# The last four tiles of experts' rows by one-hot products, and low-rank weights split ahead of time

## The chip, the cores and the metric

The kernel runs on one core of a Trainium2 chip. The metric is device time in microseconds (us), the median of several executions. Engines: TensorE (PE) multiplies matrices, VectorE (DVE), ScalarE (ACT) and GpSimd (POOL) work on elements, SyncE (SP) mostly issues DMAs. Each engine takes its instructions in the order in which they were written for it; waits between engines are semaphores. DMAs can be issued from SP, ACT and POOL.

## The reference, cut to what matters

Two blocks follow each other on 512 tokens of width 1024. The first ends with a mixture of experts: 64 experts of inner width 256, 8 for each token, and a shared expert.

```
order = argsort(e_flat); counts per expert padded to blocks of 128 rows
def expert_block(toks, ws, e):
    xb = u_pad[toks]
    hid = silu(xb @ we_gate[e]) * (xb @ we_up[e])
    return (hid @ we_down[e]) * ws[:, None]
routed = segment_sum(y_slots, slot_tok)          # back to tokens
h = h + g2 * (routed + shared)
h = rmsnorm(h, final_norm_g)
```

The second block begins with a time mix. Its decay and rate come through weights of low rank (w1, a1: 1024 to 64 each; w2, a2: 64 to 1024):

```
xn = rms_norm(h, norm_pre)
xmix = xn + (shift(xn) - xn) * mu                # six mixes
r, k, v, g = xmix[:4] @ w_in
w_pre = w0 + tanh(xw @ w1) @ w2
a = sigmoid(a0 + (xa @ a1) @ a2)
```

A recurrence over time, attention and a gated embedding follow; nothing there is changed.

## The kernel before, in words

**Precision.** Most products are made of three: a matrix is split into a high part h (a rounded copy, fp32r, made on ACT) and a low part l = matrix - h (DVE or POOL); `hilo` (L222 to L224) does this. A product is then h x h + h x l + l x h.

**First block.** `first_mix` ends with three products on the branch weights (the last is w_brp, L493) and then with w_out, which feeds the residual `hT` ([128, 8, 512], features on partitions). PE runs without a break there.

**Experts.** `Schedule` lists tiles of 128 rows: one expert, or two half experts with 64 rows each. `Experts.run` (L1303) goes over them in a pipeline: tile i's rows were gathered (POOL) and transposed (`operand`), `gate_up` makes the hidden rows, `hidden` the activation on ACT and DVE, `turned` transposes it, `down` makes 1024 outputs for each row. For most tiles `out` scales the rows by their routing weights into `m_y` and POOL scatters them, added up, to one of two token-ordered buffers in DRAM, `rt_d[0]` and `rt_d[1]`, in turn (L1248; a tile of two halves makes two scatters). A scatter waits until the scatter before it to the same buffer has landed.

A tile with `t.add` (the last two, L1092) goes another way, `parts` (L1252): its scaled rows are split into `yh` (ACT, L1264) and `yl` (DVE, L1265), and a matrix `to` of ones and zeros, from comparing row numbers, says which token each row belongs to (L1261, four instructions). `added` (L1272) multiplies (`yh`, `yl`) with `to` for every tile kept: for two tiles four products for each of the 8 feature slices, 32 in all, each slice added to `hT` by `residual` (L1269, DVE).

**The way back.** At tile N-3, `back` (L1286) issues four SP loads of the two halves of `rt_d[0]` and `rt_d[1]` (1 MB each) into places of experts' weights. Ahead of the last tile's outputs in the code the rest of it runs: DVE and POOL add the two (L1297), PE transposes 32 squares (L1301), DVE adds to `hT`. A loop for surplus blocks (L1386) runs zero times here, but engines pass its branches. After it `added(on_h)` handles the tiles kept, with `Norms.add` squaring each slice (ACT, L1430), summing (PE, L1432), storing `hT` to `h_d` and at the end making the norm factors (DVE L1438 to L1441, POOL L1442).

**Start of the second block.** `rwkv` (L1454) opens pools for its tiles; the first, `wts3`, holds three buffers each of `wr`, `wh`, `wl` (a weight as loaded, its high and its low part), and lies where experts' tiles were. `Pre.lora` (L1604) loads the low-rank weights, multiplies w1 by the mixing factors (DVE, L1623, held by `issue_after` until the norm's last DVE instruction), subtracts (L1624), splits three matrices of 128 x 1024, and then multiplies 48 times (L1633) with the normed `hT` (L1500), whose parts `xh`, `xl` come from ACT and from DVE and POOL in turn. Behind it come the mixes for k and r, `mix` (L1490), and 8 pairs of products for k and r (L1522). Between these, `Pre.stages` sets, for a pair, products on L1703, L1712, L1734 and L1742; L1742 takes `p_bk`, whose last part is DVE's L1722. The weights for these products are loaded by `weights` (L1507) into `wr`.

The code's order is not the order of the engines: the frame around the program runs its own timing of the whole and sets the instructions of each engine from it, so that a change in one stage also moves instructions in others.

## Time and profile before

| what | us |
|---|---|
| median of 3 runs | 2513.7 (2513.29 to 2515.72) |
| the profiled execution | 2504.29 |
| its span (first to last instruction) | 2502.5 |

All rows come from the profiled execution, which was 9.4 us quicker than the median. Its mean granted TensorE clock was 0.957 of full speed. A timeline's row reads: start, duration, engine, line, operation, output and inputs, how many in a row; in brackets the engine's idle time before and who ended it. Line numbers are those of the kernel before; in the new kernel everything from L492 on moves down by 3, from L1286 by 4, from L1341 by 6 and in the second block by 13 to 27.

### The profile page before, as it was taken

To read this page: it belongs to the slowest core of one execution; us is meant where nothing else is said; L and a number is where in the kernel's file an instruction comes from. 1 tells how busy PE (TensorE), PEld (TensorE's weight loads), DVE (VectorE), ACT (ScalarE), POOL (GpSimd) and SP (SyncE) were. 2 spreads that over 40 slices of the span, in tenths; PEclk is the share of its full clock that TensorE was granted. 3 is DMA by queue.
4 is the path that set the end of the run, shared out by engine and by line. 5 is a ranking of instruction groups with operands and counts; after the bars stand their busy time and mean duration, and the time that the engine had idled before them with its cause. 6 is when DMAs were issued, how large, how long until landed. Compare 5 with 4: busy or idle time off the path is not lost. (4 is left out here: it accounts for less than half of the span.)

```text
span 2502.5 us, 31640 instructions
## 1 busy us (share of the span) xinstructions
PE 2283.3 (91%) x11912; PEld 1641.4 (66%) x11912; DVE 1308.8 (52%) x2382; ACT 876.6 (35%) x1597; POOL 771.3 (31%) x596
## 2 busy tenths in 40 slices
PE   6899999998998999999989976998979899999997
PEld 3677888776886544443334335666868798988887
DVE  5567877767643433211111126758525556477765
ACT  3443333343322211111111115535326644354552
POOL 2333434114001122222212224449324221655212
PEclk9899999999999999999999987999979999999998
DMA  7232333344733889999999963576765432122211
GB/s 287 94 101 101 103 108 108 119 145 159 268 101 119 338 302 399 381 347 387 399 382 362 376 203 117 152 187 189 205 175 200 144 105 88 56 60 65 79 65 51
DMA packets 187178, 477.16 MB, mean 191 GB/s; under 512 B 62333, under 2 KB 111869, under 8 KB 146832
## 3 DMA queue, kind: packets, MB, share of 16 engines
q1 hardware_dynamic: 161392, 424.48, 47.1%
q0 software_dynamic: 16288, 37.21, 5.7%
q10 hardware_dynamic: 9344, 13.44, 1.8%
q8 instruction: 94, 1.54, 0.2%
q14 instruction: 60, 0.49, 0.1%
HBM read 423.66 MB, written 71.89 MB: 198 GB/s over the span
## 5 line engine op out<-in xcount | busy, mean ns | idle before, releaser
L224 POOL TENSOR_TENSOR wl<-wr,wh 128x1024 fp32r<-128x1024 f32 x80 | 202.9, 2553 | 373.2 <-ACT wh L223 373.2
L223 ACT ACTIVATE wh<-wr 128x1024 fp32r<-128x1024 f32 (+1 forms) x202 | 204.3, 1043 | 236.1 <-PE mm L205 147.7
L205 PE MATMUL mm<-uh,wh 128*128 128x512 f32 x640 | 258.4, 404 | 10.4 <-DVE cv L604 7.6
L205 PE MATMUL mm<-ul,wh 128*128 128x512 f32 x640 | 256.1, 400 | 0.0
L205 PE MATMUL mm<-uh,wl 128*128 128x512 f32 x640 | 255.7, 400 | 0.0
L1196 PE MATMUL mm<-m_we,m_x 128*64 128x512 f32 (+1 forms) x672 | 250.7, 599 | 0.3 <-DMA m_we<-in_w_exp_dram 0.3
L205 PE MATMUL mm<-ya,wh 128*128 128x256 f32 x1280 | 243.9, 291 | 6.8 <-ACT wh L223 6.7
L205 PEld LDWEIGHTS mm<-ya,wh 128*128 128x128 f32 x1280 | 204.9, 196 | 13.9 <-ACT wh L223 7.9
L224 DVE TENSOR_TENSOR wl<-wr,wh 128x1024 fp32r<-128x1024 f32 (+1 forms) x122 | 154.7, 1286 | 65.6 <-ACT wh L223 65.3
L205 PE MATMUL mm<-ya,wl 128*128 128x256 f32 x640 | 184.6, 289 | 0.0
L1186 DVE COPY m_x<-sm 128x512 f32<-128x512 f32 x48 | 33.2, 691 | 289.5 <-PE mm L1196 226.5
L1196 PE MATMUL mm<-m_wl,m_x 128*64 128x512 f32 (+1 forms) x432 | 169.1, 601 | 5.9 <-DMA m_wl<-in_w_exp_dram 5.9
L1196 PEld LDWEIGHTS mm<-m_we,m_x 128*64 128x64 f32 (+1 forms) x672 | 86.8, 159 | 111.4 <-issue 108.8
L1196 PE MATMUL mm<-m_we,m_ht 128*64 128x512 f32 (+1 forms) x368 | 140.8, 601 | 11.4 <-ACT m_y L1236 6.7
L205 PEld LDWEIGHTS mm<-uh,wh 128*128 128x128 f32 x640 | 122.3, 191 | 41.5 <-issue 8.1
L205 PEld LDWEIGHTS mm<-ul,wh 128*128 128x128 f32 x640 | 122.0, 191 | 29.0 <-issue 0.3
L205 PEld LDWEIGHTS mm<-uh,wl 128*128 128x128 f32 x640 | 121.7, 190 | 29.3
L1169 POOL DMA_INDIRECT m_xg<-u_d,sgi x48 | 50.4, 1050 | 273.5 <-PE sm L1184 81.1
L205 PEld LDWEIGHTS mm<-ya,wl 128*128 128x128 f32 x640 | 125.3, 196 | 0.5
L1522 PE MATMUL mm<-xh,wh 128*128 128x512 f32 x256 | 106.3, 418 | 5.7 <-ACT xh L223 3.4
L1248 POOL DMA_INDIRECT rt_d<-m_y,sgi x46 | 70.9, 1542 | 125.0 <-ACT m_y L1236 35.2
L1522 PE MATMUL mm<-xl,wh 128*128 128x512 f32 x256 | 105.6, 413 | 4.0 <-DVE xl L224 2.8
(575 smaller groups left out, 4839.9 us busy)
## 6 DMA issues: line engine op xcount, KB each, us to landing
m_we<-in_w_exp_dram SPq DMA_DIRECT2D x117, 1024.0 KB
m_wl<-in_w_exp_dram SPq DMA_DIRECT2D x78, 1024.0 KB
wr<-in_w_grp_dram SPq DMA_DIRECT2D x32, 1024.0 KB
wr<-in_w_ada_dram SPq DMA_DIRECT2D x18, 1024.0 KB
ck<-pk_d SPq DMA_DIRECT2D x16, 1024.0 KB
csb<-cs_d ACTq DMA_DIRECT2D x16, 512.0 KB
wr<-in_w_pg_dram SPq DMA_DIRECT2D x8, 1024.0 KB
raw<-in_w_ada_dram SPq DMA_DIRECT2D x6, 1024.0 KB
```

The lines of the kernel that those rows point to most:

```text
L205: nc.tensor.matmul(pt, lhsT=l, rhs=r, start=n == 0, stop=n == last)
L223: self.nc.scalar.activation(hi, src, AF.Copy)
L224: return (eng or self.nc.vector).tensor_sub(lo, src, hi.bitcast(F32)).ins
L1169: self.g.nc.gpsimd.indirect_dma_start(out=xg, out_offset=None, in_=self.u2_d, bounds_check=511, oob_is_err=False, in_offset=bass.IndirectO ...
L1186: nc.vector.tensor_copy(x[:, 4:], v_(p, 4))
L1196: self.mark = self.g.nc.tensor.matmul(p[s], lhsT=x[:, s], rhs=w, start=start, stop=stop).ins
L1248: nc.gpsimd.indirect_dma_start(out=self.rt_d[self.turn], out_offset=bass.IndirectOffsetOnAxis(ap=ix, axis=0), in_=y[:ix.shape[0]], in_offs ...
L1522: nc.tensor.matmul(p, lhsT=a_[:, s], rhs=b_, start=k == 0 and i == 0, stop=k == 7 and i == 2)
```

## The change

There are three parts. **First**, four tiles instead of two get `t.add`; when the loop is at tile N-2, ahead of the way back's second half, `added()` brings in tiles N-4 and N-3, and the list is emptied. **Second**, `lora_weights` prepares all low-rank parts in the first block, between w_brp and w_out, with POOL and ACT, and stores six matrices (0.5 MB each) to `lw_d` in DRAM from POOL; `Pre.lora` only loads them, from POOL. **Third**, `Experts.tile` gives `hid`, `ht` and `to` to the pool `wp`, and only `x` to `xp`; and in `rwkv` the pool `rp` is opened ahead of `wts3`. The places of `wr`, `wh` and `wl` are then others.

```
@@ -177,6 +177,7 @@
         self.ps = pool("ps", 1, space=PSUM)
         self.last = None
         self.e_d = self.dram.tile([2, 8, P, 512], F32, name="e_d")
+        self.lw_d = self.dram.tile([6, P, 1024], F32R, name="lw_d")
 
     def acc(self, n=512):
         return self.ps.tile([P, 512], F32, tag="mm", name="mm", bufs=3)
@@ -491,6 +492,8 @@
             g.linear(pk("w_gs"), uh, ul, on_gs)
             g.linear(pk("w_gp"), uh, ul, on_gp)
             g.linear(pk("w_brp"), mh, ml, on_yp)
+        with tc.tile_pool(name="lorw", bufs=1, reuse_waits="tile") as sp:
+            lora_weights(g, sp)
         xs = {}
         sp = st.enter_context(tc.tile_pool(name="sq", bufs=1, reuse_waits="tile", side="right"))
         sq = [sp.tile([P, 512], F32, name="sq%d" % i) for i in range(2)]
@@ -1089,7 +1092,7 @@
         for _, x in sorted(place(full) + place(three) + place(mixed), key=lambda x: x[0]):
             for y in x:
                 add(*y)
-        for t in self.tiles[-2:]:
+        for t in self.tiles[-4:]:
             t.add = True
         self.slot, self.aux = {}, aux
         keys = [t.key for t in self.tiles if t.key]
@@ -1124,7 +1127,7 @@
         self.raw, self.xg, self.us, self.turn = {}, {}, [], 0
 
     def tile(self, n, w, bufs, dt=F32):
-        return self.xp.tile([P, w], dt, tag="m_" + n, name="m_" + n, bufs=bufs)
+        return (self.xp if n == "x" else self.wp).tile([P, w], dt, tag="m_" + n, name="m_" + n, bufs=bufs)
 
     def y(self, dt=F32):
         return self.wp.tile([P, 1024], dt, tag="m_y", name="m_y", bufs=5)
@@ -1282,6 +1285,7 @@
                 if m % 2 == 0:
                     t = self.x_tile()
                 on_h(m, t[:, 512 * (m % 2):512 * (m % 2) + 512])
+        self.add = []
 
     def back(self):
 
@@ -1338,6 +1342,8 @@
             if i + 1 < N:
                 p = g.acc()
                 gate_up(p, i + 1, 0)
+            if whole and i == N - 2:
+                self.added()
             if whole and i == N - 1:
                 drain(bk)
             t = self.turned(hid)
@@ -1406,6 +1412,27 @@
     return [g.a[n][i].rearrange("p m k c -> p (m k c)") for i in range(2)]
 
 
+def lora_weights(g, sp):
+
+
+    nc, a = g.nc, g.a
+    t = lambda n, b, dt=F32: sp.tile([P, 1024], dt, tag=n, name=n, bufs=b)
+    w1, wb, w2 = t("w1", 1), t("wb", 1), t("w2", 1)
+    nc.sync.dma_start(out=w1, in_=a["w_l1"])
+    for j in range(2):
+        nc.sync.dma_start(out=w2[64 * j:64 * j + 64], in_=a["w_l2"][:, 1024 * j:1024 * j + 1024])
+    v8 = lambda x: x.rearrange("p (k c) -> p k c", k=8)
+    for j in range(2):
+        o, s = VOFF["mu"][0] + 32 + 8 * j, slice(64 * j, 64 * j + 64)
+        nc.gpsimd.tensor_mul(v8(wb)[:, :, s], v8(w1)[:, :, s], g.vecs[:, o:o + 8][:, :, None].to_broadcast([P, 8, 64]))
+    nc.gpsimd.tensor_sub(w1, w1, wb)
+    for i, r in enumerate((w1, wb, w2)):
+        h, l = t("h", 2, F32R), t("l", 2, F32R)
+        g.hilo(h, l, r, nc.gpsimd)
+        nc.gpsimd.dma_start(out=g.lw_d[2 * i], in_=h)
+        nc.gpsimd.dma_start(out=g.lw_d[2 * i + 1], in_=l)
+
+
 class Norms:
 
 
@@ -1438,7 +1465,7 @@
                 nc.vector.tensor_copy(p.rearrange("p (i c) -> p c i", i=2)[:, c], self.sums[c][:, :2])
             nc.vector.tensor_scalar(v[:, :4], p[:, :4], 1.0 / 1024, EPS, op0=OP.mult, op1=OP.add)
             nc.vector.tensor_scalar(w, v[:, :4], EPS, None, op0=OP.mult)
-            self.last = nc.vector.scalar_tensor_tensor(v[:, 4:], p[:, 4:8], 1.0 / 1024, w, op0=OP.mult, op1=OP.add).ins
+            nc.vector.scalar_tensor_tensor(v[:, 4:], p[:, 4:8], 1.0 / 1024, w, op0=OP.mult, op1=OP.add)
             nc.gpsimd.tensor_tensor(self.r, v, g.mhalf[:, 0:1].to_broadcast([P, 8]), op=OP.pow)
 
     def factor(self, i):
@@ -1471,8 +1498,8 @@
         nc.vector.memset(g.blk64[64:, 64:], 1.0 / 64)
         with contextlib.ExitStack() as s1:
             op1 = lambda n: s1.enter_context(tc.tile_pool(name=n, bufs=1, reuse_waits="tile"))
+            sp = op1("rp")
             wp = op1("wts3")
-            sp = op1("rp")
             omu = sp.tile([P, 48], F32, name="omu")
             o = VOFF["mu"][0]
             nc.vector.tensor_scalar(omu, g.vecs[:, o:o + 48], -1.0, 1.0, op0=OP.mult, op1=OP.add)
@@ -1535,7 +1562,7 @@
                 return nx
 
             p = Pre(g, op1("pre"), dr, cst, wc, pk_d, ld, td, ud, od)
-            p.lora(normed(), wp, norms.last)
+            p.lora(normed(), wp)
             xk, xr = mix(1), mix(0)
             p.rates(0)
             xv = None
@@ -1601,30 +1628,16 @@
     def t3(self, n, b=1):
         return self.sp.tile([P, 8, 128], F32, tag="p_" + n, name="p_" + n, bufs=b)
 
-    def lora(self, xs, wp, last):
+    def lora(self, xs, wp):
 
         g = self.g
         nc, a = g.nc, g.a
         self.w2h, self.w2l = self.t("w2h", 1, 1024, F32R), self.t("w2l", 1, 1024, F32R)
         self.th, self.tl = self.t("th", 1, 512, F32R), self.t("tl", 1, 512, F32R)
         wt = lambda n, b, dt=F32R: wp.tile([P, 1024], dt, tag=n, name=n, bufs=b)
-        w2 = wt("wr", 3, F32)
-        for j in range(2):
-            nc.sync.dma_start(out=w2[64 * j:64 * j + 64], in_=a["w_l2"][:, 1024 * j:1024 * j + 1024])
-        g.hilo(self.w2h, self.w2l, w2, nc.gpsimd)
-
-        w1, wb = wt("wr", 3, F32), wt("wr", 3, F32)
-        nc.sync.dma_start(out=w1, in_=a["w_l1"])
-        v8 = lambda t: t.rearrange("p (k c) -> p k c", k=8)
-        ws = []
-        with g.tc.issue_after(last):
-            for j in range(2):
-                o, s = VOFF["mu"][0] + 32 + 8 * j, slice(64 * j, 64 * j + 64)
-                nc.vector.tensor_mul(v8(wb)[:, :, s], v8(w1)[:, :, s], g.vecs[:, o:o + 8][:, :, None].to_broadcast([P, 8, 64]))
-            nc.vector.tensor_sub(w1, w1, wb)
-            for r in (w1, wb):
-                ws.append((wt("wh", 3), wt("wl", 3)))
-                g.hilo(*ws[-1], r)
+        ws = [(wt("wh", 3), wt("wl", 3)) for _ in range(2)]
+        for i, t in enumerate([t for w in ws for t in w] + [self.w2h, self.w2l]):
+            nc.gpsimd.dma_start(out=t, in_=g.lw_d[i])
         ps = [g.acc(), g.acc()]
         for k, (xh, xl) in enumerate(xs):
             s = slice(k * P, k * P + P)
```

Three places show what moves. The first is TensorE at the end of the experts. Before, the hidden rows of the last tile are made, the down products of N-2 (64-row halves) and N-1 follow, then all 32 transposes:

```order
L1196 MATMUL mm<-m_wl,m_ht 64x512
L1196 MATMUL mm<-m_we,m_ht 64x512
L1196 MATMUL mm<-m_wl,m_ht 64x512
L1213 MATMUL a_9938<-cst,m_hid 128x128 x2
L1196 MATMUL mm<-m_wl,m_ht 128x512 x4
L1301 MATMUL sm<-cst,m_we 128x128 x32
```

Now (L1282 is the product with `to`, L1305 the transpose of the way back, L1199 gate, up and down, L1216 the turn of a hidden tile) the order is:

```order
L1199 MATMUL mm<-m_wl,m_x 128x512 x8
L1282 MATMUL mm<-m_to,m_y 128x512 x12
L1216 MATMUL a_10029<-cst,m_hid 128x128 x2
L1282 MATMUL mm<-m_to,m_y 128x512 x12
L1305 MATMUL sm<-cst,m_we 128x128 x12
L1282 MATMUL mm<-m_to,m_y 128x512 x8
L1199 MATMUL mm<-m_we,m_ht 64x512
L1199 MATMUL mm<-m_wl,m_ht 64x512
L1199 MATMUL mm<-m_we,m_ht 64x512
L1199 MATMUL mm<-m_wl,m_ht 64x512
L1305 MATMUL sm<-cst,m_we 128x128 x4
L1199 MATMUL mm<-m_we,m_ht 64x512
```

What moved: 32 products on `to` (12 + 12 + 8) stand here, and the first 12 transposes of the way back stand ahead of the down products of N-2 and N-1. DVE has the same exchange: its first addition of the way back (L1301 now) stands among the eight new residuals, ahead of `to` of tile N-2.

The second place is VectorE from the norm's last instruction (L1441 before, L1468 now) to the first low part of a normed slice. Before:

```order
L1441 SCALAR_TENSOR_TENSOR m_xg<-m_xg 128x4
L1623 TENSOR_TENSOR wr<-wr,vecs 128x8x64 x2
L1581 MEMSET m_10280 128x4
L1590 MEMSET half 128x1
L1595 TENSOR_SCALAR hv<-vecs 128x8 x3
L1583 MEMSET m_10280 32x1 x4
L1624 TENSOR_TENSOR wr<-wr 128x1024
L1500 SCALAR_TENSOR_TENSOR hT<-hT,gain,sm 128x512 x8
L224 TENSOR_TENSOR wl<-wr,wh 128x1024 x2
L224 TENSOR_TENSOR xl<-hT,xh 128x512
```

Now:

```order
L1468 SCALAR_TENSOR_TENSOR m_xg<-m_xg 128x4
L1608 MEMSET m_10371 128x4
L1617 MEMSET half 128x1
L1622 TENSOR_SCALAR hv<-vecs 128x8
L1610 MEMSET m_10371 32x1 x4
L1622 TENSOR_SCALAR hv<-vecs 128x8 x2
L1527 SCALAR_TENSOR_TENSOR hT<-hT,gain,sm 128x512 x8
L225 TENSOR_TENSOR xl<-hT,xh 128x512
L1517 SCALAR_TENSOR_TENSOR mx<-hT,vecs,mx 128x511 x2
```

What moved: the two products on L1623, the difference on L1624 and the two `wl` on L224 are gone from in front of `hT` and `xl`.

On GpSimd, four of the loads of `lw_d` stand right behind the surplus blocks' loop, ahead of `nrm` (L1442 before, L1469 now); the two for `p_w2h` and `p_w2l` stand behind the six memsets (L1587, L1588) that follow `nrm`, where GpSimd made `p_w2l` itself before. On SyncE the first loads of weights for k and r (L1507 before, L1534 now: two of w_ak, one of w_ar) stand right behind the loop now, ahead of the stores of `h_d`. ScalarE makes the high part of the first of them among the squares of the norm, and VectorE its low part between the fourth and the fifth residual.

The third place is TensorE in the second of the 8 pairs of k and r, from one pair's L1734 to its L1742 (L1747 and L1755 now). Before:

```order
L1712 MATMUL sm<-cst,p_u 64x128 x8
L1734 MATMUL sm<-p_k_10740,p_brk 128x512
L1522 MATMUL mm<-xl,wh 128x512
L1522 MATMUL mm<-xh,wl 128x512
L1522 MATMUL mm<-xh,wh 128x512
L1522 MATMUL mm<-xl,wh 128x512
L1522 MATMUL mm<-xh,wl 128x512
L1742 MATMUL sm<-ab_10287,p_bk 128x128 x8
```

Now:

```order
L1725 MATMUL sm<-cst,p_u 64x128 x8
L1747 MATMUL sm<-p_k_10822,p_brk 128x512
L1549 MATMUL mm<-xh,wl 128x512
L1549 MATMUL mm<-xh,wh 128x512
L1549 MATMUL mm<-xl,wh 128x512
L1549 MATMUL mm<-xh,wl 128x512
L1664 MATMUL rate<-p_th,p_w2h 128x512
L1664 MATMUL rate<-p_tl,p_w2h 128x512
L1664 MATMUL rate<-p_th,p_w2l 128x512
L1755 MATMUL sm<-ab_10378,p_bk 128x128 x8
```

What moved: seven instructions of other products stand between where five stood; over the eight pairs the numbers of k and r products there were 0, 5, 3 and 3 at first before, and are 0, 4, 17, 13, 12, 7, 24 and 31 now.

## Rows read from the trace of the kernel before

**Rows 1.** The page: span and instructions.

```profile
span 2502.5 us, 31640 instructions
```

**Rows 2.** Windows: busy us of each engine, granted clock, DMA share, GB/s.

```profile
core 0: us, PE busy (x) PEld busy (x) DVE busy (x) ACT busy (x) POOL busy (x), PEclk, DMA share, GB/s
1480.00:1500.00 20.00, 6.31 (x26) 4.71 (x25) 8.30 (x9) 0.69 (x1) 5.76 (x2) 0.59 0.61 212
1520.00:1540.00 20.00, 5.82 (x18) 4.04 (x18) 15.29 (x32) 10.02 (x15) 16.26 (x14) 0.53 0.55 191
```

**Rows 3.** Timeline of TensorE, from the experts' end to the low-rank products.

```profile
1491.16 1.97 PE L1301 MATMUL sm<-cst,m_we 128*128 128x128 f32 x8 [10.28 <-DVE m_we L1297]
...
1504.31 5.45 PE L1279 MATMUL mm<-m_to,m_y 128*128 128x512 f32 x16 [2.15 <-issue]
...
1523.19 1.12 PE L1449 MATMUL sm<-cst,nrm 128*128 128x128 f32 x4 [2.68 <-POOL nrm L1442]
1531.52 1.22 PE L1633 MATMUL mm<-xh,wh 128*128 128x512 f32 x2 [7.21 <-ACT xh L223]
1537.04 0.80 PE L1633 MATMUL mm<-xl,wh 128*128 128x512 f32 x1 [4.30 <-DVE xl L224]
```

**Rows 4.** Timeline of GpSimd: scatters (L1248) and the way back (L1297).

```profile
1466.87 1.56 POOL L1248 DMA_INDIRECT rt_d<-m_y,sgj  x1 [6.36 <-DMA rt_d<-m_y,sgi]
...
1473.30 1.57 POOL L1248 DMA_INDIRECT rt_d<-m_y,sgj  x1 [3.13 <-DMA rt_d<-m_y,sgj]
...
1489.90 3.41 POOL L1297 TENSOR_TENSOR m_we<-m_we 128x1024 f32<-128x1024 f32 x1 [13.18 <-DMA m_we<-rt_d]
1494.98 2.34 POOL L1297 TENSOR_TENSOR m_we<-m_we 128x1024 f32<-128x1024 f32 x1 [1.67 <-DMA m_we<-rt_d]
```

**Rows 5.** Timeline of SyncE: the way back's loads.

```profile
1481.16 2.38 SPq L1292 DMA_DIRECT2D m_we<-rt_d  x4
```

**Rows 6.** Timeline of VectorE at the experts' end.

```profile
1481.64 0.75 DVE L1265 SCALAR_TENSOR_TENSOR m_y<-mm,ssw,m_y 128x512 fp32r<-128x512 f32 x1 [0.97 <-ACTq L1386]
1489.88 1.22 DVE L1297 TENSOR_TENSOR m_we<-m_we 128x1024 f32<-128x1024 f32 x1 [7.49 <-DMA m_we<-rt_d]
...
1496.05 2.36 DVE L1297 TENSOR_TENSOR m_we<-m_we 128x1024 f32<-128x1024 f32 x1
1499.64 3.31 DVE L1269 SCALAR_TENSOR_TENSOR hT<-sm,mod,hT 128x512 f32<-128x512 f32 x4 [1.23 <-PE sm L1301]
```

**Rows 7.** View of L1261 by itself: making `to`; count, min/median/max ns.

```profile
L1261 DVE TENSOR_SCALAR m_to<-iota,m_tf x8: 274/294/559, 1428.9 to 1430.9; 128x128 fp32r<-128x128 bf16 x8
```

**Rows 8.** Timeline of VectorE at the start of the second block.

```profile
1525.61 1.29 DVE L1623 TENSOR_TENSOR wr<-wr,vecs 128x512 f32<-128x512 f32 x2 [4.29 <-DMA wr<-in_w_l_dram]
...
1527.56 1.29 DVE L1624 TENSOR_TENSOR wr<-wr 128x1024 f32<-128x1024 f32 x1
1528.77 5.34 DVE L1500 SCALAR_TENSOR_TENSOR hT<-hT,gain,sm 128x512 f32<-128x512 f32 x8
1534.03 2.35 DVE L224 TENSOR_TENSOR wl<-wr,wh 128x1024 fp32r<-128x1024 f32 x2
...
1544.27 1.21 DVE L224 TENSOR_TENSOR wl<-wr,wh 128x1024 fp32r<-128x1024 f32 x1
```

**Rows 9.** Timeline of GpSimd there.

```profile
1521.46 1.68 POOL L1442 TENSOR_TENSOR nrm<-m_xg,mhalf 128x8 f32<-128x8 f32 x1 [24.13 <-DVE m_xg L1441]
...
1527.98 3.09 POOL L224 TENSOR_TENSOR p_w2l<-wr,p_w2h 128x1024 fp32r<-128x1024 f32 x1
```

**Rows 10.** TensorE's waits from 1560 to 1860 us: total, times, longest.

```profile
PE sm L1742 <- DVE p_bk L1722: 6.3, 4, 2.4
PE rate L1651 <- ACT p_rate L1654: 3.7, 3, 1.5
```

**Rows 11.** Timeline of GpSimd, 797 to 803 us: idle until then, four plain DMA issues.

```profile
797.32 0.95 POOL L1157 MEMSET m_y<- 128x1024 f32 x1 [179.27 <-PE mm L205]
...
800.09 2.50 POOL L1159 DMA_DIRECT2D rt_d<-m_y  x4
```

More of the change, by code (lines that the diff above doesn't have):

```diff
@@ L179, in __init__ @@
         self.e_d = self.dram.tile([2, 8, P, 512], F32, name="e_d")
+        self.lw_d = self.dram.tile([6, P, 1024], F32R, name="lw_d")
     def acc(self, n=512):
@@ L493, in first_mix @@
             g.linear(pk("w_brp"), mh, ml, on_yp)
+        with tc.tile_pool(name="lorw", bufs=1, reuse_waits="tile") as sp:
+            lora_weights(g, sp)
         xs = {}
@@ L1091, in __init__ @@
                 add(*y)
-        for t in self.tiles[-2:]:
+        for t in self.tiles[-4:]:
             t.add = True
@@ L1284, in added @@
                 on_h(m, t[:, 512 * (m % 2):512 * (m % 2) + 512])
+        self.add = []
     def back(self):
@@ L1340, in run @@
                 gate_up(p, i + 1, 0)
+            if whole and i == N - 2:
+                self.added()
             if whole and i == N - 1:
@@ L1406, in pk, with lora_weights @@
     return [g.a[n][i].rearrange("p m k c -> p (m k c)") for i in range(2)]
+def lora_weights(g, sp):
+    nc, a = g.nc, g.a
+    t = lambda n, b, dt=F32: sp.tile([P, 1024], dt, tag=n, name=n, bufs=b)
+    w1, wb, w2 = t("w1", 1), t("wb", 1), t("w2", 1)
+    nc.sync.dma_start(out=w1, in_=a["w_l1"])
+    for j in range(2):
+        nc.sync.dma_start(out=w2[64 * j:64 * j + 64], in_=a["w_l2"][:, 1024 * j:1024 * j + 1024])
+    v8 = lambda x: x.rearrange("p (k c) -> p k c", k=8)
+    for j in range(2):
+        o, s = VOFF["mu"][0] + 32 + 8 * j, slice(64 * j, 64 * j + 64)
+        nc.gpsimd.tensor_mul(v8(wb)[:, :, s], v8(w1)[:, :, s], g.vecs[:, o:o + 8][:, :, None].to_broadcast([P, 8, 64]))
+    nc.gpsimd.tensor_sub(w1, w1, wb)
+    for i, r in enumerate((w1, wb, w2)):
+        h, l = t("h", 2, F32R), t("l", 2, F32R)
+        g.hilo(h, l, r, nc.gpsimd)
+        nc.gpsimd.dma_start(out=g.lw_d[2 * i], in_=h)
+        nc.gpsimd.dma_start(out=g.lw_d[2 * i + 1], in_=l)
 class Norms:
@@ L1440, in add @@
             nc.vector.tensor_scalar(w, v[:, :4], EPS, None, op0=OP.mult)
-            self.last = nc.vector.scalar_tensor_tensor(v[:, 4:], p[:, 4:8], 1.0 / 1024, w, op0=OP.mult, op1=OP.add).ins
+            nc.vector.scalar_tensor_tensor(v[:, 4:], p[:, 4:8], 1.0 / 1024, w, op0=OP.mult, op1=OP.add)
             nc.gpsimd.tensor_tensor(self.r, v, g.mhalf[:, 0:1].to_broadcast([P, 8]), op=OP.pow)
@@ L1537, in rwkv @@
             p = Pre(g, op1("pre"), dr, cst, wc, pk_d, ld, td, ud, od)
-            p.lora(normed(), wp, norms.last)
+            p.lora(normed(), wp)
             xk, xr = mix(1), mix(0)
@@ L1602, in t3, with lora @@
         return self.sp.tile([P, 8, 128], F32, tag="p_" + n, name="p_" + n, bufs=b)
-    def lora(self, xs, wp, last):
+    def lora(self, xs, wp):
         g = self.g
@@ L1610, in lora @@
         wt = lambda n, b, dt=F32R: wp.tile([P, 1024], dt, tag=n, name=n, bufs=b)
-        w2 = wt("wr", 3, F32)
-        for j in range(2):
-            nc.sync.dma_start(out=w2[64 * j:64 * j + 64], in_=a["w_l2"][:, 1024 * j:1024 * j + 1024])
-        g.hilo(self.w2h, self.w2l, w2, nc.gpsimd)
-        w1, wb = wt("wr", 3, F32), wt("wr", 3, F32)
-        nc.sync.dma_start(out=w1, in_=a["w_l1"])
-        v8 = lambda t: t.rearrange("p (k c) -> p k c", k=8)
-        ws = []
-        with g.tc.issue_after(last):
-            for j in range(2):
-                o, s = VOFF["mu"][0] + 32 + 8 * j, slice(64 * j, 64 * j + 64)
-                nc.vector.tensor_mul(v8(wb)[:, :, s], v8(w1)[:, :, s], g.vecs[:, o:o + 8][:, :, None].to_broadcast([P, 8, 64]))
-            nc.vector.tensor_sub(w1, w1, wb)
-            for r in (w1, wb):
-                ws.append((wt("wh", 3), wt("wl", 3)))
-                g.hilo(*ws[-1], r)
+        ws = [(wt("wh", 3), wt("wl", 3)) for _ in range(2)]
+        for i, t in enumerate([t for w in ws for t in w] + [self.w2h, self.w2l]):
+            nc.gpsimd.dma_start(out=t, in_=g.lw_d[i])
         ps = [g.acc(), g.acc()]
```

4 lines of the change are left out of this document (2 added, 2 removed).

## The prediction

> **What bounds the kernel now.** I read the page's busy slices first, then windows, then the timeline of one engine after another where TensorE has gaps. Over most of the span of 2502.5 us [rows 1] TensorE is busy without a break and nothing the change touches there can be seen at the end; so I looked for places where it stands still near the edited lines. The windows show two: from 1480 to 1500 it is busy for 6.31 us of 20, from 1520 to 1540 for 5.82 of 20, and the granted clock has fallen to 0.59 and 0.53 [rows 2]. In the first, TensorE waits 10.28 us for the way back's first addition and 2.15 us more at the branch of the surplus loop; in the second, 2.68 us for the norm factors, 7.21 us for the first `xh` and 4.30 us for the first `xl` [rows 3].
>
> The first gap is a chain through DRAM. The last scatters of tile N-3 have to land before SyncE can issue the way back's four loads at 1481.16 [rows 5]; the first two have landed at 1489.88, when VectorE starts to add, and the third and fourth at 1494.98, when GpSimd's second addition ends its wait [rows 4, 6]. So two loads take 8.72 us and four 13.82, that is 2.55 us for each 1 MB and 3.6 us besides. The stage's end is VectorE's last addition to `hT`, 1499.64 + 3.31 = 1502.95 [rows 6].
>
> The second gap is on VectorE. Its queue holds two products on the low-rank weight, which wait 4.29 us for a load, then a difference, and behind these the normed `hT`, though the norm factors were on TensorE from 1523.19 + 1.12 = 1524.31 on. `hT` starts at 1528.77. Two `wl` (2.35 us) then stand ahead of the first `xl`, a third (1.21 us) further on [rows 3, 8].
>
> **First part: four tiles by products.** Three scatters go, the last ones. The way back now waits only for the scatters up to tile N-5. The last of these starts at 1466.87 and has landed by 1473.30, when the next scatter to its buffer stops waiting [rows 4]. Its buffer is `rt_d[1]`; the scatters to `rt_d[0]` are one earlier in turn, so that its load is already out by then. The load of `rt_d[1]` goes at 1473.3, and with 1 MB ahead of the rest the first pair is there 3.6 + 2.55 = 6.2 us later, at L = 1479.5 (with all of 8.72 us, at 1482.0). Before, L was 1489.88.
>
> But more work stands behind it now. VectorE, in its order after L: the additions 1.22 + 2.36; five of the eight new residuals (three stand ahead of L) at 0.75, 3.75; eight residuals of the way back at 3.31/4 = 0.83, 6.6; two times four instructions for `to` at 0.294, 2.35; four `yl` at 0.75, 3.0 [rows 6, 7]. Sum 19.3, with 0.9 for small hand-overs 20.2. TensorE's list is as long: GpSimd's first addition, 3.41 [rows 4], then 32 transposes at 1.97/8, 7.9 [rows 3], eight to-products at 5.45/16 = 0.34, 2.7, and the down products of two tiles, about 5. So the stage ends at 1479.5 + 20.2 = 1499.7 instead of 1502.95: -3.3 us. The 24 other to-products (8.2 us) lie in the old gap ahead of L. Also ahead of L, `yl` of tile N-4 stands behind the hidden rows of N-2 on VectorE; that holds TensorE about 2 us and is covered by the wait for L. Bounds: -6 if the hand-overs and the half clock go as well; +7 if L stays near 1490 (below). The final 32 to-products and the norm stay as they are, 16 us, give or take 1.5: the first `wl` of the k weight now stands among their residuals and its load is issued right behind the loop.
>
> **Second part: low-rank weights made ahead.** What it adds lies in the first block between w_brp and w_out: GpSimd has nothing to do for 179.27 us before 797.32 there [rows 11], and its six operations are some 14 us at the durations for such shapes (2 x 1.3 for halves, four at 2.5 to 3.1 [rows 8, 9]); ScalarE's three copies of about 1 us stand between copies of weights for w_out that TensorE needs later. TensorE is the bound there and its list is unchanged: 0, at most +1 if the first expert's weights wait for the new tiles' places. If that cover were gone it would cost the 14 us.
>
> What it removes: VectorE's 4.29 us of waiting, two products and a difference. `hT` can start at 1524.4, -4.4 us. Then two `wl`, -2.35, and the third, -1.21: 8.0 us earlier for the last `xl` of the k mix [rows 8]. The four loads of `lw_d` ahead of `nrm` are issued at the loop, 20 us before TensorE wants them, and 3.5 MB (these and three weights) at the 2.55 us above take 9 to 13 us. The two later loads put 2 x 0.62 us (four issues in 2.50 [rows 11]) on GpSimd ahead of its `xl`, where 3.09 us of `p_w2l` go [rows 9]. So GpSimd isn't late for its half of the `xl`. Bounds: -4.4 if only the waiting goes, -9 if a part of the half clock goes with it.
>
> Here a rule of the Trainium skill speaks against the change: "SBUF — State Buffer", section "SBUF: two separate sides", says that a DMA from GpSimd's queue needs descriptors which GpSimd can't write while VectorE runs certain copies, 620 ns alone against about 3100 ns beside one. By it the two later issues would take 6.2 us instead of 1.25, GpSimd's `xl` would be some 3 us late, and the sum would be -9 instead of -12. The four issues of rows 11 agree with its smaller figure; no row shows such an issue beside a busy VectorE.
>
> **Third part: places.** The tiles `wr`, `wh`, `wl` no longer wait for the experts' small tiles, so the first k weights are ready early. That changes the order of the k and r products. TensorE loses 6.3 us there on L1742 (four waits, the longest 2.4) and 3.7 on the rates (three, the longest 1.5) [rows 10]. Now more products stand between L1734 and L1742 (0, 4, 17, 13, ... for 0, 5, 3, 3), which gives VectorE more time for `p_bk`; against this, other things slide. I take -1, between -5 and +4; the end of it is +21 (below).
>
> **Sum.** -3.3 - 8.0 - 1 + 0.3 for the early stage = -12.0 us. The profiled execution took 2504.3 us, so 2492.3; the runs' median is 9.4 us above it, and I carry that over: 2513.7 - 12.0 = 2501.7, say 2502.
>
> **The rivals.**
> (A) Both parts pay as above: 2502, from 2496 (-6, -9, -3) to 2508.
> (B) Only the low-rank part pays in part, the tail ends as late as before: -4.4 to -8, 2506 to 2509. For it speaks that VectorE's and TensorE's lists behind L are both near 20 us; a bit more in either eats the 3.3.
> (C) The loads of `rt_d` land as late as now, L = 1490: since the scatters' chain is slower than I read, or the loads share the DMA engines with expert weights. Then 1490 + 20.2 = 1510.2, +7.2 us, against -8.0: 2513, no change. For it: scatters wait 3 to 6 us for each other already [rows 4]. Against: what they wait for is landed by 1473.30, and weights for the last tiles are all in by then.
> (D) Slower: the new order of k and r puts the longest waits of today on each of the eight pairs, 8 x (2.4 + 1.5) = 31.2 instead of 10.0, +21. With -11 from the rest that is +10, 2524. It decides from the point where those waits grow by more than 11 us in all. For it: the order there was set by a timing of the whole with the operands early, and `p_bk` can still be late on a VectorE that is as busy as before. Against: more products between.
> (E) That the change does nothing at the end, since what is saved is waited for later (a load of `v`, say): within 5 us of zero.
>
> **How the numbers follow.** A 0.56, B 0.14, C 0.13, E 0.08, D 0.09. What can be told from no change is 0.2%, 5.0 us. A and nearly all of B are faster by more: 0.69. C, E and the rest of B: 0.22. D: 0.09. The range to hold 8 in 10 goes from A's low end with some for an unlooked-for gain, 2494, to C's 2513. For A alone it is 2496 to 2508.
>
> **What would show it.** Right: the way back's loads issued near 1473 and VectorE's first addition near 1480; the gap of 10.28 us filled with to-products; the last tile's `yl` near 1500; `hT` starting 0.1 us behind the norm factors, the first `xl` 6 us behind that, and about 11 us earlier than now in all; less than 10 us of waits on L1742 and the rates. Wrong: a first addition after 1485 (C), TensorE waiting for GpSimd's `xl` (the slow issues), waits in the k and r stage above 20 us (D), or a wait before 800 us on the new stores.

## The result, and the profile after

The changed kernel takes 2483.0 us (median of 4 runs, 2478.7 to 2486.4) against 2513.5 for the kernel before: ratio 0.9892, 95% interval [0.9875, 0.9909], by the ratio about 27 us faster. Two later series gave 0.9921 [0.9906, 0.9935] and 0.9907 [0.988, 0.9934]. The forecast was -12 us and 2502 us, so the direction was right, and the forecast size was less than half of the measured one. The profiled execution took 2480.3 us, 24.0 less than that of before [rows 1]:

```profile
span 2478.5 us, 31762 instructions
```

The windows, in the form of [rows 2], show TensorE busy for 17.73 us where it was for 6.31, and for 15.38 where it was for 5.82. The granted clock between 1480 and 1500 is 1.00 instead of 0.59 (the same stretch holds somewhat later work now):

```profile
1480.00:1500.00 20.00, 17.73 (x85) 10.74 (x84) 19.08 (x31) 3.14 (x5) 5.71 (x2) 1.00 0.38 143
1500.00:1520.00 20.00, 16.01 (x100) 13.88 (x100) 9.72 (x32) 6.01 (x9) 5.52 (x9) 0.91 0.93 338
1520.00:1540.00 20.00, 15.38 (x55) 11.84 (x56) 18.14 (x21) 11.77 (x20) 13.05 (x13) 0.75 0.23 80
```

TensorE's timeline answers to [rows 3]. In place of the wait of 10.28 us stand the new products (L1282) without a break; the first 8 transposes follow at once, and 0.98 us for GpSimd's addition is all that is left of that wait. Behind the loop the 16 products take 4.12 us, not 5.45. The first `xh` and `xl` are waited for 1.50 and 3.65 us:

```profile
1478.28 3.35 PE L1282 MATMUL mm<-m_to,m_y 128*128 128x512 f32 x12
...
1481.60 3.02 PE L1282 MATMUL mm<-m_to,m_y 128*128 128x512 f32 x12
1484.46 1.03 PE L1305 MATMUL sm<-cst,m_we 128*128 128x128 f32 x8
1486.48 0.66 PE L1305 MATMUL sm<-cst,m_we 128*128 128x128 f32 x4 [0.98 <-POOL m_we L1301]
...
1500.77 4.12 PE L1282 MATMUL mm<-m_to,m_y 128*128 128x512 f32 x16 [2.07 <-DVEq L1392]
...
1518.35 1.11 PE L1476 MATMUL sm<-cst,nrm 128*128 128x128 f32 x4 [2.69 <-POOL nrm L1469]
1520.97 1.22 PE L1646 MATMUL mm<-xh,wh 128*128 128x512 f32 x2 [1.50 <-ACT xh L224]
1525.84 0.79 PE L1646 MATMUL mm<-xl,wh 128*128 128x512 f32 x1 [3.65 <-DVE xl L225]
```

On SyncE the first of the way back's loads is issued at 1472.71 and the other three from 1477.28 on [rows 5: 1481.16 for the first]. By the code's order the first is that of `rt_d[0]`, the second that of `rt_d[1]`:

```profile
1472.71 0.39 SPq L1296 DMA_DIRECT2D m_we<-rt_d  x1
1477.28 1.48 SPq L1296 DMA_DIRECT2D m_we<-rt_d  x3
```

The forecast's 1473.3 was for the load of `rt_d[1]`, so 1472.71 is not a hit: it is the other load. Since the first block ends 5.1 us later in this trace (table below), 1477.28 stands for 1472.2 on the clock of before, 1.1 us ahead of the forecast. In the same way the last `yl` "near 1500" is met at 1500.2 only because of those 5.1 us.

On VectorE the way back's first addition (L in the prediction) starts at 1482.97 [rows 6: 1489.88], the last `yl` ends at 1500.2, a `wl` stands among the norm's residuals, and `hT` [rows 8] starts 0.04 us after the norm factors are out:

```profile
1482.97 1.23 DVE L1301 TENSOR_TENSOR m_we<-m_we 128x1024 f32<-128x1024 f32 x1 [0.56 <-DMA m_we<-rt_d]
...
1499.49 0.73 DVE L1268 SCALAR_TENSOR_TENSOR m_y<-mm,ssw,m_y 128x512 fp32r<-128x512 f32 x1
...
1508.46 1.23 DVE L225 TENSOR_TENSOR wl<-wr,wh 128x1024 fp32r<-128x1024 f32 x1 [2.78 <-ACT wh L224]
...
1519.50 5.36 DVE L1527 SCALAR_TENSOR_TENSOR hT<-hT,gain,sm 128x512 f32<-128x512 f32 x8 [2.35 <-PE sm L1476]
```

On GpSimd [rows 9] the loads for `p_w2h` and `p_w2l` stand where `p_w2l` was made:

```profile
1521.51 0.59 POOL L1640 DMA_DIRECT2D p_w2h<-lw_d  x1
1522.10 0.54 POOL L1640 DMA_DIRECT2D p_w2l<-lw_d  x1
```

VectorE is in the eight `hT` products then (1519.50 to 1524.86), and each issue takes as long as one of [rows 11] (2.50/4). "SBUF — State Buffer", section "SBUF: two separate sides", of the Trainium skill gives about 3100 ns beside certain copies; beside these products its smaller figure, 620 ns, holds. They are not copies, so this run does not test the larger figure.

TensorE's waits from 1560 to 1860 us, as in [rows 10]: shorter on the rates, longer on `p_bk`, 10.1 us in all instead of 10.0.

```profile
PE sm L1755 <- DVE p_bk L1735: 8.3, 3, 7.3
...
PE rate L1664 <- ACT p_rate L1667: 1.8, 2, 1.5
```

Cut at the same instructions in both traces, the stages last:

| stage, us | before | after | forecast difference | measured |
|---|---|---|---|---|
| start to the end of w_out | 797.3 | 802.3 | +0.3 | +5.1 |
| to the way back's first addition | 692.6 | 680.6 | -10.4 | -12.0 |
| to the first product of the last two tiles | 14.4 | 17.8 | +7.1 | +3.4 |
| to the norm factors (`nrm`) | 17.1 | 15.9 | 0 | -1.2 |
| to the normed `hT` | 7.3 | 2.9 | -4.4 | -4.4 |
| to the last low-rank product | 21.6 | 19.4 | -3.6 with the next | -2.2 |
| to the first L1742 of the 8 pairs | 47.9 | 44.6 | | -3.3 |
| to the last L1742 | 151.0 | 146.9 | -1 | -4.1 |
| to the end of the k and r products | 76.3 | 75.5 | 0 | -0.8 |
| to the start of VectorE's last instruction | 668.3 | 667.8 | 0 | -0.5 |
| to the span's end | 8.6 | 4.8 | 0 | -3.8 |

(The forecast's low-rank term ended at the last `xl` of the k mix, which lies between two of these marks. The last stage but one is edited by none of the kernels here, and it lasts 664.4 to 673.0 us in the 18 profiles: the total of a single profile moves by several us without any edit.)

### The profile page after: what moved, and what is told of

It is laid out like the page before. It is cut to its first block, busy times and chain, and to the rows that moved or that the text cites. A ratio compares the mean times of both kernels' runs of the same rounds, so it can differ in the third digit from the quotient of the medians.

```text
span 2478.5 us, 31762 instructions
## 1 busy us (share of the span) xinstructions
PE 2285.5 (92%) x11944; PEld 1646.8 (66%) x11944; DVE 1308.0 (53%) x2397; ACT 877.3 (35%) x1599; POOL 779.0 (31%) x610
## 5 line engine op out<-in xcount | busy, mean ns | idle before, releaser
L224 ACT ACTIVATE wh<-wr 128x1024 fp32r<-128x1024 f32 (+1 forms) x200 | 202.3, 1044 | 225.2 <-PE mm L206 148.1
L1199 PE MATMUL mm<-m_we,m_x 128*64 128x512 f32 (+1 forms) x672 | 250.9, 599 | 0.1
L1199 PE MATMUL mm<-m_wl,m_x 128*64 128x512 f32 (+1 forms) x432 | 169.1, 602 | 5.9 <-DMA m_wl<-in_w_exp_dram 5.9
L1199 PEld LDWEIGHTS mm<-m_we,m_x 128*64 128x64 f32 (+1 forms) x672 | 86.9, 159 | 111.2 <-issue 107.6
L1199 PE MATMUL mm<-m_we,m_ht 128*64 128x512 f32 (+1 forms) x368 | 141.2, 601 | 12.3 <-ACT m_y L1239 6.7
L1208 ACT ACTIVATE m_hid<-mm 128x256 f32<-128x256 f32 x52 | 20.0, 384 | 245.1 <-PE mm L1199 245.1
L1199 PEld LDWEIGHTS mm<-m_wl,m_x 128*64 128x64 f32 (+1 forms) x432 | 57.2, 158 | 74.4 <-issue 68.1
```

The source lines that it names most:

```text
L224: self.nc.scalar.activation(hi, src, AF.Copy)
L1199: self.mark = self.g.nc.tensor.matmul(p[s], lhsT=x[:, s], rhs=w, start=start, stop=stop).ins
```

## The experiments

Every ratio is to the kernel before; us of gain are the ratio's. "Norm" is the stage from the first product of the last two tiles to `nrm`.

**Operands' places alone.**

```
-            omu = sp.tile([P, 48], F32, name="omu")
+            omu = sp.tile([P, 56], F32, name="omu")[:, :48]
```

> The kernel before with one table (omu) 32 bytes wider, so that xh and xl move up by 32 bytes against wh and wl; every instruction and the order are the same. Theory of the address: in the trace of the changed kernel the products of the k, r, v, g stage follow each other every 227 ns, before every 232 to 233, and what differs is that the two operands' places now leave the same remainder by 64 bytes. Then this kernel has 227 ns there too, and 816 products x 5 to 6 ns = 4 to 5 us less. Rival (what surrounds the products, as other engines or DMAs, or the region of the memory, sets their pace): 232 to 233 ns as before, no change in the time.

1.0004 [0.9993, 1.0016]. The products of k and r did get quicker, as in the changed kernel. The view of their line (min, median, max in ns), first before, then this kernel, then after:

```profile
L1522 PE MATMUL mm<-xh,wh x181: 392/396/802, 1599.9 to 1799.8; 128*128 128x512 f32 x181
```

```profile
L1522 PE MATMUL mm<-xh,wh x177: 387/389/799, 1601.1 to 1799.7; 128*128 128x512 f32 x177
```

```profile
L1549 PE MATMUL mm<-xh,wh x192: 387/389/799, 1605.3 to 1799.6; 128*128 128x512 f32 x192
```

So the theory of the address was right about the pace, but the time isn't less for it: quicker products alone bring nothing here. The stage of the pairs, where TensorE waits for other engines, is 152.7 us in this trace and 151.0 before.

**First part alone.**

```
-        for t in self.tiles[-2:]:
+        for t in self.tiles[-4:]:
...
+        self.add = []
...
+            if whole and i == N - 2:
+                self.added()
```

> Only the first part: four tiles by products, added() at tile N-2. The forecast's term: the stage from the last expert rows to the last product on `to` ends 3.3 us earlier, by rows 1 of the sum; the trace of the changed kernel against a base drift of 5.3 us in the first block says 8 to 10 us. So by the forecast -3, by the trace -9; if the tail's gain needs the places of the small tiles as well, near 0.

0.9974 [0.9959, 0.9988], -6.5 us, between -3.0 and -10.3: the interval holds the -9 and just about the -3.3. The stages up to the norm are 682.8 and 19.3 (after 680.6 and 17.8), the norm 15.8. Part of the wait for the way back is still there, and the 16 products behind the loop run at full clock all the same:

```profile
1486.14 1.09 PE L1302 MATMUL sm<-cst,m_we 128*128 128x128 f32 x8 [1.79 <-DVE m_we L1298]
1488.36 0.67 PE L1302 MATMUL sm<-cst,m_we 128*128 128x128 f32 x4 [1.13 <-POOL m_we L1298]
...
1504.12 4.14 PE L1279 MATMUL mm<-m_to,m_y 128*128 128x512 f32 x16 [1.99 <-DVEq L1389]
```

**Second part alone.**

```
+            lora_weights(g, sp)
...
-    def lora(self, xs, wp, last):
+    def lora(self, xs, wp):
...
+            nc.gpsimd.dma_start(out=t, in_=g.lw_d[i])
```

> Only the second part: low-rank weights made ahead. The forecast's term: -8.0 us between the norm factors and the first products of k and r. Rival: the loads wait for the places of wh and wl, which in the kernel before lie where expert tiles were, and come late: then under -4.

0.9951 [0.9934, 0.9967], -12.3 us; once more, below, 0.9936. That is more than the forecast's -8.0 and speaks against the rival (under -4).

**The exchange of two pools alone** (from the third part).

```
+            sp = op1("rp")
             wp = op1("wts3")
-            sp = op1("rp")
```

> Only the exchange of the two pools in rwkv (half of the third part). The forecast had -1 between -5 and +4 for all of what the third part does to the k and r products. By the theory of the address this alone gives 4 to 5 us (227 ns a product), by the theory of the order only what the waits of the k and r stage (23 us before, 20 in the changed kernel) change, 3 us or so, at 232 to 233 ns.

0.9981 [0.997, 0.9992], -4.8 us. The stage of the pairs is 147.3, as in the changed kernel, so this exchange alone has that gain; waits on `p_bk` and the rates are 6.4 in that stage against 9.3 before. The products are as quick as in the first experiment, which gained nothing by it, so the new order is what is left; no run shows it by itself.

**Filled wait in the kernel before.** 28 products that nobody reads (fillers).

```
             if whole and i == N - 1:
+                for _ in range(7):
+                    q, (y0, _, to0) = g.acc(), self.add[0]
+                    for j in range(4):
+                        g.nc.tensor.matmul(q, lhsT=y0[:, j * P:j * P + P], rhs=to0, start=j == 0, stop=j == 3)
                 drain(bk)
```

> The kernel before with 28 products more, whose result nobody reads (a tile's rows by `to`, again), on TensorE ahead of the last tile's down products, in the 10 us in which it waits for the way back. Nothing comes earlier by it; what it changes is that TensorE works in that wait. Theory of the clock: the granted clock falls to half at 1483 in the kernels with two tiles and, in three of four of their traces, a second time in the norm behind (from `to` products to `nrm` 20.5 to 21.9 us, in one 17.1), and stays full to 1516 in the kernels with four tiles (15.8 and 15.9). Then this kernel takes 16 us there and is 3 to 5 us quicker than before. Rival (the norm's time hangs on what comes earlier or on DMAs): 17 to 22 us as before, and the time unchanged or up to 1 us longer.

0.9989 [0.9978, 1.0001]. The granted clock rises and the norm is 15.7 us, with the order of its instructions on TensorE unchanged. The same window of before and of this kernel:

```profile
1500.00:1520.00 20.00, 17.85 (x104) 15.66 (x102) 9.23 (x18) 5.06 (x8) 0.00 (x0) 0.81 0.28 95
```

```profile
1500.00:1520.00 20.00, 15.33 (x100) 13.40 (x99) 8.69 (x22) 6.12 (x9) 1.82 (x2) 0.93 0.45 155
```

The price of the clock shows in the norm of this trace, but the kernel's time is not told from that of before: the filled wait gives 2.8 us, between a gain of 5.5 and a loss of 0.3.

**One load from GpSimd instead of SyncE in the kernel before.**

```
-            nc.sync.dma_start(out=cst, in_=a["rcst"])
+            nc.gpsimd.dma_start(out=cst, in_=a["rcst"])
```

> The kernel before with one load (rcst, 0.46 MB) issued from GpSimd instead of SyncE behind the surplus loop; all else and the order are the same. In the traces so far GpSimd's last drain at the program's end takes 8.3 us where its last DMAs are the scatters, and 4.3 to 4.6 where loads of lw_d come behind them, and the program's end waits for it. Theory: any plain DMA from GpSimd behind the scatters does it: 3.5 to 4 us less. Rival: it hangs on something else in the second part (the number of its DMAs, the place of the output in DRAM): no change.

1.0000 [0.9987, 1.0013], no gain of 3.5 us. The end of the span shrank as in the changed kernel (4.8 instead of 8.6 us) without a gain in time; in this trace the norm took 21.7 and the pairs 156.2, more than in that of before. Whether the 3.8 us of the changed kernel's end are a gain is therefore not shown.

**The change without its second part** (the diff of "second part alone", backwards).

```
-            lora_weights(g, sp)
...
+        with g.tc.issue_after(last):
```

> The changed kernel without its second part: four tiles by products, and the places. By the sum of the parts measured one by one (0.9974 and 0.9981) 0.9955. From the last gathered rows to the last `to` products the changed kernel was 8.6 us quicker than before, the first part alone 5.0: if the places of `to` are what the tail lacks, this one has 8 to 9 us there; if it hangs on the order that the low-rank part changes, 5. No gain at the program's drain.

0.9991 [0.9981, 1.0001]: nearly the whole gain is gone, and the expected 0.9955 is missed. Ahead of the transposes TensorE waits again, and the 16 products behind the loop run in part at half clock; the norm is 21.2:

```profile
1484.12 1.09 PE L1302 MATMUL sm<-cst,m_we 128*128 128x128 f32 x8 [2.03 <-DVE m_we L1298]
1486.34 1.02 PE L1302 MATMUL sm<-cst,m_we 128*128 128x128 f32 x4 [1.12 <-POOL m_we L1298]
...
1502.11 5.54 PE L1279 MATMUL mm<-m_to,m_y 128*128 128x512 f32 x16 [1.98 <-DVEq L1389]
```

The waits of 2.03 and 1.12 us don't explain it: the first part alone has 1.79 and 1.13 there, the change without its third part (below) 1.94 and 1.12, and in both the 16 products take 4.14 us and the norm 15.8 and 16.9. This profile's span (2500.9 us) is also no longer than that of the first part alone (2502.0), and the two ratios' intervals overlap. What takes the gain away is open.

**The change with a pad of 32 bytes**, which by the tiles' sizes sets the first block's operands to the same remainder of their addresses by 64 bytes.

```
+        pad = st.enter_context(tc.tile_pool(name="rpad", bufs=1, reuse_waits="tile", side="right")).tile([P, 8], F32, name="rpad")
+        nc.vector.memset(pad, 0.0)
```

> The changed kernel with 32 bytes of padding ahead of the first block's weights, so that the two operands of its 2544 products of 512 columns (uh, mh, yh, ph by wh, wl) start at the same remainder by 64 bytes; same order. In the first block TensorE is busy without a break from 600 to 797 us and in most of the time before. Theory of the address (232 to 234 ns a product become 227, as in e1): where TensorE is the bound 6 to 7 ns x 2544 = 15 to 18 us less. Rival: as in e1, where the pace fell and the time did not: something else bounds it too, no change; or the pace stays at 234 since it was the region and not the remainder.

0.9904 [0.9883, 0.9925]: not to be told from the change. The expected 15 to 18 us aren't there. Sixty us of the first block hold 261 products against 252, and w_out ends at 793.5 instead of 802.3 (797.3 before). But part of this is the clock, which was 0.98 in that stretch of the changed kernel; in the kernel before, at 1.00 as here, it is 256. Before, after, then this kernel:

```profile
620.00:680.00 60.00, 59.63 (x256) 47.58 (x256) 45.66 (x75) 21.47 (x29) 0.00 (x0) 1.00 0.78 275
```

```profile
620.00:680.00 60.00, 59.63 (x252) 47.57 (x251) 47.69 (x80) 20.14 (x27) 2.74 (x2) 0.98 0.75 270
```

```profile
620.00:680.00 60.00, 59.62 (x261) 48.63 (x260) 45.76 (x75) 21.75 (x29) 0.00 (x0) 1.00 0.79 285
```

**The change without its first part.**

```
-        for t in self.tiles[-4:]:
+        for t in self.tiles[-2:]:
...
-            if whole and i == N - 2:
-                self.added()
```

> The changed kernel with two tiles kept instead of four, that is without the first part. The theory of the clock: with two tiles TensorE waits 10 us for the way back, the granted clock falls to half there and again in the norm, 20 to 22 us from the `to` products to `nrm`; so this kernel loses the 8.6 us of the tail and 4 to 6 of the norm against the changed one and comes out 13 to 15 us above it, at 0.994 to 0.995 of before. By the single parts (0.9951 and 0.9981) 0.993. Rival (parts that add up as in the forecast): the loss is the forecast's 3.3 us, 0.990 to 0.991.

0.999 [0.9974, 1.0006]; once more, below, 0.9978. The norm takes 25.2 us. Neither expectation held: the loss is larger than both.

**The change without its third part, and the change again.**

```
-        return (self.xp if n == "x" else self.wp).tile([P, w], dt, tag="m_" + n, name="m_" + n, bufs=bufs)
+        return self.xp.tile([P, w], dt, tag="m_" + n, name="m_" + n, bufs=bufs)
...
-            sp = op1("rp")
             wp = op1("wts3")
+            sp = op1("rp")
```

> The changed kernel without its third part (small tiles where they were, wts3 ahead of rp). By the single parts 0.9974 x 0.9951 = 0.9925. If the clock stays full through the tail and the norm, as in the changed kernel, those two stages are 16 us and 6 to 9 us better than before and what is lost is the pools' exchange alone, 4 to 5 us: 0.991. If the tail's wait for the way back opens again (as in the kernel without the second part), 0.994.

> The changed kernel once more, to be compared in the same call with the others and to see how far its stages repeat: 0.989, norm at 16 us.

Both 0.9921, [0.9907, 0.9934] and [0.9906, 0.9935]: with the other two in, the third part gives nothing that can be told, though its exchange of pools alone gave 4.8 us. Without it the norm is 16.9 us and the pairs' stage 150.3.

**The change with the pad and with 17 products nobody reads in the waits ahead of `xl`.**

```
+            if k == 0:
+                q = g.acc()
+                for j in range(14):
+                    nc.tensor.matmul(q, lhsT=ws[0][0][:, j % 8 * P:j % 8 * P + P], rhs=xh, start=j == 0, stop=j == 13)
...
+            for j in range(3):
+                nc.tensor.matmul(q[:, P:], lhsT=t[:, P:2 * P], rhs=t[:, P:], start=j == 0, stop=j == 2)
```

> The changed kernel with the 32 bytes of padding of e8 and with 17 products more whose result nobody reads: 3 between the norm's sums and `nrm`, 14 behind the first `xh`, where TensorE waits 2.7 and 3.7 us. Theory of the clock: the half clock from 1516 to 1530 goes or is shorter, the 14 low-rank products at 0.63 us run at 0.39, 3 to 4 us less up to the end of the low-rank stage; together with the padding's 3 to 8 us in the first block 0.985 to 0.987. Rival: the clock stays low in spite of the filling, or what follows waits for VectorE anyway (the mixes end with it): 0.988 to 0.990, as the changed kernel.

0.9914 [0.9901, 0.9927], no better. The clock did rise: nearly all low-rank products take 0.39 us. But from `nrm` to the last of them it is 22.4 us, as in the changed kernel (22.3), with 1.83 us of waiting for VectorE's `xl` in between, as the rival said; the time is above both expectations. The way from the last low-rank product to the first pair is 52.2 us instead of 44.6, with other products in another order there; why it costs so much is open.

**Does the clock link the parts?** The change without its first part, with the fillers of the fifth experiment in the open wait; the same without them; the second part alone; the change; all timed together.

```
+                for _ in range(7):
+                    q, (y0, _, to0) = g.acc(), self.add[0]
...
                 drain(bk)
```

> The second and third parts without the first, and 28 products more (nobody reads them) on TensorE ahead of the last tile's down products, where it waits 10 us for the way back. If the lost clock is what made these two parts alone worth only 2.5 us (norm stage 25.2 us), the norm stage is 16 +/- 1 us here and the ratio lies 0.002 to 0.005 below that of the same kernel without the products in this call. If the clock is worth nothing at the end: the same ratio within 0.0015.

> The second and third parts alone, once more. If 0.999 was this kernel's own time: 0.9975 to 1.0005, norm stage over 20 us. If it was the scatter of one call: about 0.994, the two parts' single gains.

> The second part alone, once more, beside the kernel with the third part too. If single ratios repeat: 0.9935 to 0.9965. If the scatter of one call is as large as such gains: anything from 0.993 to 0.999, with a norm stage that differs from the 21.8 us seen.

> The whole change once more, for the scale of this call: 0.989 to 0.993, norm stage 15.9 to 17.1 us, full clock until 1515 us or later.

In this order 0.992 [0.9902, 0.9939], 0.9978 [0.9966, 0.999], 0.9936 [0.9916, 0.9956] and 0.9907 [0.988, 0.9934]. The fillers bring back 0.0058 (14.6 us), more than I expected, and the norm is 19.5 us, not 16. The clock doesn't explain that: from 1500 to 1520 and from 1520 to 1540 us it was 0.71 and 0.59 without fillers, 0.74 and 0.58 with them, and the 16 products behind the loop run in part at half clock in both traces, without and with fillers (4.12 us in the changed kernel):

```profile
1508.27 5.66 PE L1282 MATMUL mm<-m_to,m_y 128*128 128x512 f32 x16 [2.09 <-issue]
```

```profile
1507.95 6.25 PE L1282 MATMUL mm<-m_to,m_y 128*128 128x512 f32 x16 [1.94 <-issue]
```

What differs is the order, of TensorE's sums and of VectorE. Without fillers the `wl` of the first k weight stands behind the second residual and waits for a weight that was asked for at the loop's end, and TensorE's sums pile up behind it; with fillers it stands behind the fourth. Without, then with fillers:

```profile
1516.76 1.23 DVE L225 TENSOR_TENSOR wl<-wr,wh 128x1024 fp32r<-128x1024 f32 x1 [3.91 <-ACT wh L224]
```

```profile
1515.70 1.23 DVE L225 TENSOR_TENSOR wl<-wr,wh 128x1024 fp32r<-128x1024 f32 x1 [0.72 <-ACT wh L224]
```

With fillers the norm is 6.1 us shorter, and the pairs' stage 5.9 (145.9 against 151.8). The two profiles as a whole differ by 6.6 us only, as the stage that nobody edits is 8.6 us longer in the one with fillers. So this run doesn't show the clock to be the link; it points to the order, which the fillers moved too. No run changes the place of that `wl` alone. The price of the clock alone is best seen between two profiles of one and the same kernel, the second part alone: the last 24 sums of the norm, in its first and its second series, and the norm with them 21.8 and 18.3 us. The granted clock from 1505 to 1530 was 0.67 and 0.77:

```profile
1521.59 5.11 PE L1456 MATMUL nsum<-ngain,m_xg 128*128 128x2 f32 x24
```

```profile
1521.56 2.73 PE L1456 MATMUL nsum<-ngain,m_xg 128*128 128x2 f32 x24
```

## Why the prediction was wrong

The mechanism was rival A's: no wait took the place of the old one, and C and D didn't happen. The steps that failed are sizes, and one assumption about the profile. Between the two profiles the change is worth 24.0 us, not 12.0; the largest pieces of the difference are the list of work behind L (3.7 us), the end of the span (3.8) and the third part (3.1), against an early stage that lost 4.8 us more than was said. By the prediction's steps:

1. **First part, "-3.3 us".** L came at 1482.97, but in a run whose first block was 5.1 us later; from there L is 12.0 earlier, where 10.4 was said: right. The list behind it was mis-sized: 17.8 us, not 20.2 with its hand-overs. A residual takes 0.69 us (2.06 for 3), not 0.75 to 0.83, when several stand together and none waits for TensorE; the second addition takes 1.21, not 2.36; and instead of 0.9 for hand-overs, the instructions' times overlap by about 1 us in all. Against this the eight instructions for `to` took 3.7 us, not 2.35. TensorE's own list ran at full clock (8 transposes in 1.03 us, not 1.97). So the term is -8.6 in these two profiles. In the time of the part alone it is -6.5, whose interval reaches from -10.3 to -3.0, and there the list took 19.3 us. The bound "-6 if the hand-overs and the half clock go as well" was nearer than the value taken.
2. **"The final 32 to-products and the norm stay as they are, 16 us, give or take 1.5".** To `nrm` 15.9 came after 17.1; to TensorE's last sum, which the 16 us fit, 14.9 after 16.2. But the step took [rows 3] for typical. Five profiles of kernels with the same order on TensorE there and the old wait in front have 18.3 to 21.9 to `nrm` (the first, the third twice, the fourth and the sixth experiment), 20.2 on average with the 17.1 of before. With more products in front of it, it is 15.8 (first part alone), 16.9 (without the third part), 15.9, 17.1 and 17.3 (three profiles of the change), though 21.2 in the kernel without the second part. So by these averages some 3 us were to be had in the median, which the profile of before didn't show.
3. **Second part, "-8.0".** From `nrm` to the first pair it is -9.9: -4.4 for `hT` as worked out, -5.5 for the rest against 3.6. In time the part alone gave -12.3 and -16.1 (0.9936), beyond its bound of -9. The end of the span is 3.8 us shorter in it too, which no step had; the sixth experiment doesn't bear this out as a gain, so some 2 to 6 us of this part stay unexplained.
4. **Third part, "-1".** -4.1 in the stage of the pairs, and the exchange of pools alone shows the same (-3.7). The waits that the prediction summed went from 10.0 to 10.1 us and would have said nothing; 7.3 of them are now one wait. Better placed operands made each product 7 ns shorter (396 to 389), but the first experiment shows no gain from that alone. So the gain comes with the new order, and which instruction of it pays isn't settled.
5. **"The runs' median is 9.4 us above it, and I carry that over".** This made up about a third of the miss in the predicted time (9.4 - 2.7 of 19 us). The profile of before was a quick execution of its kernel: later runs of it took 2501 to 2518 us, with medians of 2509 to 2514. The profiled executions of the change were 2.7, 4.2 and 0.6 us below their medians. What was 9.4 us for before was not a property that the changed kernel keeps.
6. **"+ 0.3 for the early stage".** w_out ended 5.1 us later (801.9 to 802.3 in the three profiles of the change; 796.2 to 799.0 in five that hold neither the first nor the second part). The loss was real and the step too small. The new work ahead of w_out isn't all of it: the first part alone, which adds nothing there, has 802.1 too, and the second part alone 799.1 and 801.0. Some of the loss lies in the first 100 us, where TensorE made 231 to 235 products in the change (233 with the first part alone) instead of 240 to 244. Its cause isn't settled.

Whether parts add: alone they give 6.5 + 12.3 (or 16.1) + 4.8 = 24 to 27 us, with only the exchange of pools measured of the third part; the whole gives 20 to 27. But two of the three kernels with one part taken out fall short of such sums. Without the first part a `wl` waits 4 us among the residuals; that this is the cause was not tested. Without the second the cause is open. The second and third parts together (0.999 and 0.9978) are worth less than the second alone (0.9951 and 0.9936), clear of the intervals both times.

## What to carry to other kernels

Where TensorE waits behind a chain through DRAM, the wait can cost twice: by itself, and by the half clock of what follows. Here the second is seen in the stages, not surely in the kernel's time. Look for the same stage in more than one profile before calling its length typical, and don't carry a profile's distance from the median over to another kernel. When instructions are reordered by the whole program's timing, an experiment that takes one part out also makes a new order: compare the order around the waits first, then the times. Look, too, where an engine waits for a transfer that was asked for only a few us earlier: here a `wl` held up VectorE for 3.91 us between two residuals.

## What the runs showed of the hardware

- The same 128x512 product took a median of 396 ns, and 389 with one table ahead of `xh` 32 bytes wider and no other edit. By the tiles' sizes 224 bytes stand ahead of `xh` in its pool before and 256 then, so that `xh` and `wh` have different remainders of their addresses by 64 bytes before (32 and 0) and equal ones then. In the first block 32 bytes of padding go with 261 products in 60 us against 256 in the kernel before, at a granted clock of 1.00 in both. A gain in the kernel's time isn't shown for either.
- GpSimd's last step before the program's end is longer where no plain DMA went through its queue behind the last scatter: from its start to the span's end 9.2 us before and 5.3 after. It holds in all 18 profiles: from VectorE's last instruction to the span's end it is 8.4 to 8.6 us in the six without such a DMA and 4.8 to 4.9 in the twelve with one or more. The chain's last row, of before and after:

```profile
2493.33 1.52 POOLq L2467
```

```profile
2473.25 1.52 POOLq L2480
```

One load moved to GpSimd's queue did the same in the sixth experiment (4.8 instead of 8.6 us behind VectorE's last instruction). Why is open, and so is whether the kernel gains by it.
